# Four of eight experts with unsplit float32 weights, two products side by side on TensorE

## The chip, the cores and the metric

The kernel runs on one core of one Trainium2 chip. The metric is the time of one execution on the device in microseconds (us); before the change the median of three runs is 2477.5 us.

## What is computed

The reference is a network of two layers over 256 latent tokens with 1024 channels, behind 256 context tokens. Each layer has a normalised, modulated input, three token mixers, an output projection, and then a SwiGLU stage: dense in the first layer, eight experts of which each token takes two in the second. All arrays are float32. The change touches only the expert stage of the second layer, which works on the 256 latent tokens:

```
D_MODEL, D_FF_EXPERT, N_EXPERTS, TOP_K = 1024, 2816, 8, 2

def swiglu(h, w_gate, w_up, w_down):
    return (jax.nn.silu(h @ w_gate) * (h @ w_up)) @ w_down

def moe_swiglu(h, w_router, w_gate, w_up, w_down):
    logits = h @ w_router
    top_v, top_i = lax.top_k(logits, TOP_K)
    top_w = jax.nn.softmax(top_v, axis=-1)
    combine = jnp.sum(jax.nn.one_hot(top_i, N_EXPERTS) * top_w[..., None], axis=-2)
    out = combine[..., 0:1] * swiglu(h, w_gate[0], w_up[0], w_down[0])
    for e in range(1, N_EXPERTS):
        out = out + combine[..., e:e + 1] * swiglu(h, w_gate[e], w_up[e], w_down[e])
    return out
```

A residual with a gate row and a last norm follow.

## The kernel before

**Ranks and slots.** The router's code (from L1160 on) counts the tokens of each expert and puts the experts in the order of falling counts: rank 0 has most tokens. The counts of all ranks add up to 512. `posr` holds for each token and rank its slot, `comr` its factor, `eidi` the expert of a rank, `cnti` the counts. The kernel works by rank, with a fixed number of slots for each: 128 + 64 for rank 0, 128 for ranks 1 to 4, 64 for ranks 5 to 7.

**Float32 by split parts.** A float32 value is split into a high and a low part of a narrower type (fp32r in the profile), whose sum is the value: `split` (L111) has ScalarE (ACT) write the high part as a copy (L114) and VectorE (DVE) the low part as a difference (L115). A block of 128 slots is multiplied with a block of weights by three products on TensorE (PE): high by high, high by low of the weights, low of the tokens by high. A block of 64 slots holds both parts of its tokens side by side, 128 columns in all, so two products do: by the weights' high and by their low part. One such sweep over an expert's weights is called a pass below.

**Weights.** They lie in memory in blocks ("units") of 128 rows x 1024 float32, 512 KB: two blocks of 128 rows by 512 columns. An expert has 22 units each of gate, up and down, 66 in all, and the eight experts 528. `raw` (L117) asks for a unit on SP's DMA queue (L119) into one of six places; `weight` (L122) splits it into one of three pairs of places (`wh`, `wl`). A place is free again when its last reader is done: that of a raw unit after the split, that of a pair after PE's products.

**The order.** `slots` (L1250) gathers tokens into slots: it makes one-hot matrices on DVE, turns them on PE (L1268), and multiplies (L1279, and L1297 for rank 0's mixed block). `stream` (L1306) walks a product block by block: per block of 512 columns one PSUM bank for each slot block, per unit of weights the products of L1322, then a yield. `expert` (L1329) calls it for gate (bank names `eg`), up (`eu`) and down (`ed`); what follows the last unit of a bank is SiLU on ACT, the product with up on DVE, four transposes on PE (L1370) and a split for down; after down a split, the products that put the slots back to the tokens (L1393, "combine") and DVE's addition to the sum `eacc` (L1395). `moe` (L1198) runs ranks 1 and 2, 3 and 4, 5 and 6, and 7 through `others` (L1232). From the 264th unit on (`EVERY`), rank 0's generator is advanced by one unit after every third one of the others, and what is left of it comes last. Names in the profile carry the rank: `edr1` is the down product of rank 1, `eg0` to `ed0` are rank 0's. The scheduler keeps to the order of the code, but puts work under `prio("w")` (requests and splits of weights) far ahead and work under `prio("ev")` (what follows a finished bank) somewhat ahead. Each engine then works through its own list in order; a wait stops all that stands behind it on that engine.

**The end.** `final` (L1400) makes the residual and the norm. Then three tests (L1218, L1219) each load one count, of ranks 1, 5 and 0, and compare it with the slots of that rank; code for the surplus tokens stands behind each and is run only where there are any.

## Time and profile before

| | |
|---|---|
| three runs | 2478.45, 2477.50, 2477.01 us; median 2477.5 |
| span of the profiled execution | 2472.9 us, 33330 instructions |
| its own time | not measured apart from its span |
| PE busy | 2379.4 us, 96%, 11759 products |
| DVE busy | 1808.8 us, 73% |
| ACT busy | 1338.7 us, 54% |
| POOL busy | 20.3 us, 1% |
| DMA | 469.69 MB, 190 GB/s over the span |

The profile is of one execution; its span runs from the first to the last instruction and leaves out what lies around them, which the runs' times hold. Busy is the time in which an engine has an instruction under way; products on PE overlap in the records, so a row's duration is longer than the step to the next row. PE's granted clock is at full speed in nearly all of the span.

### The profile page before, as it was taken

Reading aid. Unit: us, or ns where it says so; the run is one execution under the profiler, and the core shown is the slowest. Engines: PE = TensorE matmul, PEld = TensorE weight load, DVE = VectorE, ACT = ScalarE, POOL = GpSimd, SP = SyncE. Lnnn points to the kernel's source line nnn. Section 1 sums busy time; section 2 is a strip of 40 time slices with the busy share of each in tenths; the row PEclk is TensorE's granted clock in tenths of the full one; section 3 lists DMA queues with packets and bytes.
Section 4 is the critical chain, followed back from the end, with each engine's and each line's share of the span. In section 5 each row is a group of like instructions: output and inputs, shape, how many; then the busy total and the mean of one; then the engine's idle time right before and its main releaser. Section 6 shows DMA issues by size and latency. Waiting matters only on the chain.

```text
span 2472.9 us, 33330 instructions
## 1 busy us (share of the span) xinstructions
PE 2379.4 (96%) x11759; PEld 1809.5 (73%) x11759; DVE 1808.8 (73%) x2655; ACT 1338.7 (54%) x2047; POOL 20.3 (1%) x30
## 2 busy tenths in 40 slices
PE   7999999999998999999999999989999999999995
PEld 3475476778787777777877789867788787767774
DVE  3285696574456677765798867688899888888986
ACT  3133454854434222223536676467777778788874
POOL 0000000000000000000000000000000000000000
PEclk9999999999999999999999999989999999999998
DMA  7533431112243555543332333479999999999994
GB/s 270 155 94 102 146 101 51 52 52 86 85 141 94 155 167 159 162 137 111 105 99 80 112 98 117 145 267 356 346 333 359 343 333 335 349 323 335 342 328 169
DMA packets 144334, 469.69 MB, mean 190 GB/s; under 512 B 15760, under 2 KB 16272, under 8 KB 144144
## 3 DMA queue, kind: packets, MB, share of 16 engines
q1 hardware_dynamic: 143296, 464.71, 54.6%
q10 hardware_dynamic: 848, 2.62, 0.3%
q8 instruction: 98, 1.61, 0.3%
q14 instruction: 92, 0.75, 0.1%
HBM read 466.22 MB, written 1.05 MB: 189 GB/s over the span
## 4 chain that ended last, share of the span: by engine, by line
PE 77%; DVE 10%; DMA 4%; ACT 4%; issue 3%; POOL 0%; SPq 0%; POOLq 0%; DVEq 0%; ACTq 0%
PE eur L1322 7%; PE edr L1322 7%; PE egr L1322 6%; DMA adaw<-in_ada_w_dram 3%; PE wg L179 3%; PE wg L181 2%; PE wg L180 2%; PE ada L318 2%; PE xbcL L180 2%; PE eu L1322 2%; PE xbcL L179 2%; PE xbcL L181 2%; PE ed L1322 1%; PE eg L1322 1%; DVE adac L343 1%
## 5 line engine op out<-in xcount | busy, mean ns | idle before, releaser
L115 DVE TENSOR_TENSOR l_eur<-r_eur,h_eur 128x1024 fp32r<-128x1024 f32 x154 | 185.4, 1221 | 27.3 <-ACT h_eur L114 26.8
L115 DVE TENSOR_TENSOR l_edr<-r_edr,h_edr 128x1024 fp32r<-128x1024 f32 x154 | 186.4, 1222 | 21.4 <-ACT h_edr L114 14.3
L115 DVE TENSOR_TENSOR l_egr<-r_egr,h_egr 128x1024 fp32r<-128x1024 f32 x154 | 186.2, 1220 | 12.0 <-ACT h_egr L114 10.2
L114 ACT ACTIVATE h_edr<-r_edr 128x1024 fp32r<-128x1024 f32 x154 | 162.3, 1059 | 52.3 <-PE edr L1322 28.1
L114 ACT ACTIVATE h_egr<-r_egr 128x1024 fp32r<-128x1024 f32 x154 | 162.3, 1059 | 31.5 <-PE eur L1322 19.1
L114 ACT ACTIVATE h_eur<-r_eur 128x1024 fp32r<-128x1024 f32 x154 | 160.7, 1056 | 23.5 <-PE egr L1322 9.7
L343 DVE SCALAR_TENSOR_TENSOR adac<-adaw,sc,adac 128x512 f32<-128x512 f32 x168 | 118.5, 746 | 41.7 <-DMA adaw<-in_ada_w_dram 41.2
L1322 PE MATMUL egr<-l_egr,gHp 128*128 128x512 f32 (+1 forms) x336 | 131.3, 393 | 4.0 <-DVE l_egr L115 3.7
L179 PE MATMUL wg<-hHm,h_wg 128*128 128x512 f32 (+1 forms) x384 | 132.5, 346 | 0.0
L1322 PE MATMUL eur<-l_eur,gHp 128*128 128x512 f32 (+1 forms) x336 | 129.0, 387 | 2.3 <-DVE l_eur L115 1.9
L181 PE MATMUL wg<-hHm,l_wg 128*128 128x512 f32 (+1 forms) x384 | 130.7, 343 | 0.1
L180 PE MATMUL wg<-hLm,h_wg 128*128 128x512 f32 (+1 forms) x384 | 130.0, 339 | 0.0
L1322 PE MATMUL egr<-h_egr,gHp 128*128 128x512 f32 (+1 forms) x336 | 125.7, 376 | 1.1 <-ACT h_egr L114 1.1
L1322 PE MATMUL edr<-l_edr,hHr 128*128 128x512 f32 x308 | 123.2, 400 | 3.0 <-DVE l_edr L115 1.7
L1322 PE MATMUL eur<-h_eur,gHp 128*128 128x512 f32 (+1 forms) x336 | 125.3, 376 | 0.7 <-ACT h_eur L114 0.7
L1322 PE MATMUL edr<-h_edr,hHr 128*128 128x512 f32 x308 | 121.3, 394 | 0.0
L115 DVE TENSOR_TENSOR l_wg<-r_wg,h_wg 128x1024 fp32r<-128x1024 f32 x48 | 58.8, 1224 | 42.9 <-ACT h_wg L114 42.1
L526 DVE SCALAR_TENSOR_TENSOR ccv<-cu,cols,ccv 128x482 f32<-128x482 f32 (+14 forms) x120 | 84.9, 729 | 0.7
L1322 PEld LDWEIGHTS egr<-l_egr,gHp 128*128 128x128 f32 x336 | 63.2, 188 | 28.7 <-DVE l_egr L115 19.7
L1322 PEld LDWEIGHTS eur<-l_eur,gHp 128*128 128x128 f32 x336 | 63.2, 188 | 26.4 <-DVE l_eur L115 16.5
L179 PEld LDWEIGHTS wg<-hHm,h_wg 128*128 128x128 f32 x384 | 72.8, 190 | 10.0 <-issue 2.8
L181 PEld LDWEIGHTS wg<-hHm,l_wg 128*128 128x128 f32 x384 | 72.4, 189 | 9.7 <-issue 1.6
(664 smaller groups left out, 6567.3 us busy)
## 6 DMA issues: line engine op xcount, KB each, us to landing
r_egr<-in_moe_gate_dram SPq DMA_DIRECT2D x154, 512.0 KB, 5.2
r_eur<-in_moe_up_dram SPq DMA_DIRECT2D x154, 512.0 KB, 5.3
r_edr<-in_moe_down_dram SPq DMA_DIRECT2D x154, 512.0 KB, 5.1
adaw<-in_ada_w_dram SPq DMA_DIRECT2D x160, 256.0 KB, 3.0
r_wg<-in_w_in_dram SPq DMA_DIRECT2D x48, 512.0 KB, 3.5
r_xbcL<-in_w_in_dram SPq DMA_DIRECT2D x24, 512.0 KB, 3.5
r_fg<-in_ffn_gate_dram SPq DMA_DIRECT2D x22, 512.0 KB, 3.4
r_fu<-in_ffn_up_dram SPq DMA_DIRECT2D x22, 512.0 KB, 3.5
```

Source lines behind the costliest of these rows:

```text
L114: nc.scalar.activation(Hd, src, AF.Copy)
L115: nc.vector.tensor_tensor(Ld, src, Hd.bitcast(F32), op=ALU.subtract)
L179: mm(out, wh, xh, start=(first and kk == 0), stop=False, skip_group_check=True)
L180: mm(out, wh, xl, start=False, stop=False, skip_group_check=True)
L181: mm(out, wl, xh, start=False, stop=(kk == kc - 1), skip_group_check=True)
L318: nc.tensor.matmul(ps[32 * j:32 * j + 32, :], self.sc[:, k, :], w[j % 2], start=(k == 0), stop=(k == KD - 1), skip_group_check=True)
L343: nc.vector.scalar_tensor_tensor(d, w, c, d, op0=ALU.mult, op1=ALU.add)
L526: nc.vector.scalar_tensor_tensor(y[:, :, a:b], x[:, :, a + s:b + s], w[:, k:k + 1], y[:, :, a:b], op0=ALU.mult, op1=ALU.add)
L1322: mm(ps[j][:, :n], st[kk], w[p][:, k, :], start=(kk == 0 and q == 0), stop=(kk == kc - 1 and q == len(ops) - 1), skip_group_check=True)
```

## The change

Ranks 4 to 7 leave the path of split weights. Rank 4 gets 64 slots in place of 128.

* `slots64` (L1274 of the changed kernel) makes and turns one-hot matrices as `slots` does, gathers all four blocks of 64 slots at once, with one product of 256 columns in place of one for each block, and keeps the tokens as float32 (`xn`).
* `expert64` (L1305) multiplies them with the raw units as they arrive, in float32 and without a split. A block of 64 tokens fills 64 columns of PE's array. So gate's product goes to the partitions 0 to 63 of one PSUM bank (name `nn`) and up's to 64 to 127, in turns; for down the two halves of the 1024 output columns take these places (`nd`). One piece of such an expert, up to a yield, is a unit of gate and one of up, or two units of down: four such half-products (eight in the two pieces of the last block of 256 columns). An expert has 33 pieces and 140 half-products, the four together 132 and 560. Behind a bank follow ACT's copy (`nt`, L1332), four transposes (`np`, L1335), SiLU (`ns`, L1338) and DVE's product; behind down a split and the combine with four additions.
* `moe` runs two generators by turns: `wide` (rank 0 first, then ranks 1, 2 and 3) and `narrow` (ranks 4 to 7). While rank 0's 66 units last, a turn is two wide units and two narrow pieces, then three and one (`TURN`).
* There are eight raw places, not six, and five PSUM banks for accumulation in place of four, which leaves three for the rest (the banks of `pw`), not four.
* The count gets a ninth column, the largest surplus over all ranks, and one outer test of it stands around the three tests.
* A scratch area for DMA gets the size 1024; the comments are dropped.

528 units are split before and 264 after. The number of units that are asked for stays 528, on the same queue. The engines' lists are the same up to the expert stage's gathers.

The diff, without the comments that it drops:

```diff
-        cn, self.cnti = tl(NE), self.cst.tile([128, NE], I32, name="cnti")
+        cn, self.cnti = tl(NE + 1), self.cst.tile([128, NE + 1], I32, name="cnti")
         nc.vector.tensor_tensor(c1, pm, cnt[:, None, :].to_broadcast(sq), op=ALU.mult)
-        nc.vector.tensor_reduce(cn, c1, axis=AX.X, op=ALU.add)
+        nc.vector.tensor_reduce(cn[:, 0:NE], c1, axis=AX.X, op=ALU.add)
+        caps = tl(NE)
+        for v, cap in ((caps[:, 0:1], 192.0), (caps[:, 1:4], 128.0), (caps[:, 4:NE], 64.0)):
+            nc.gpsimd.memset(v, cap)
+        nc.vector.tensor_tensor(caps, cn[:, 0:NE], caps, op=ALU.subtract)
+        nc.vector.tensor_reduce(cn[:, NE:NE + 1], caps, axis=AX.X, op=ALU.max)
+        nc.vector.tensor_scalar(cn[:, NE:NE + 1], cn[:, NE:NE + 1], 0.0, None, op0=ALU.max)
         nc.vector.tensor_copy(self.cnti, cn)
...
     def moe(self):
...
-        r0 = largest()
-        n = 0
-        for _ in self.others((((1, 0, 128), (2, 0, 128)), ((3, 0, 128), (4, 0, 128)), ((5, 0, 64), (6, 0, 64)), ((7, 0, 64),))):
-            n += 1
-            if n >= self.EVERY[0] and (n < self.EVERY[0] + KD or (n - self.EVERY[0]) % self.EVERY[1] == 0):
-                next(r0, None)
-        for _ in r0:
+        near = []
+        xw = []
+        for _ in self.slots("0", ((0, 0, 128), (0, 128, 64)), "g0", xw):
             pass
+        for _ in self.slots64("n", tuple((r, 0) for r in range(4, NE)), near):
+            pass
+        def wide():
+            yield from self.expert("0", 0, xw, "eh")
+            yield from self.others((((1, 0, 128), (2, 0, 128)), ((3, 0, 128),)))
+        def narrow():
+            for r, x in zip(range(4, NE), near):
+                yield from self.expert64(f"n{r}", r, x)
+        w, n = wide(), narrow()
+        left = FF // 128 * 3
+        while True:
+            a, b = self.TURN[0] if left > 0 else self.TURN[1]
+            more = [next(w, None) for _ in range(a)] + [next(n, None) for _ in range(b)]
+            left -= a
+            if all(m is None for m in more):
+                break
         self.final()
-        for lim, blocks in ((1, ((1, 128, 128), (2, 128, 128))), (5, ((5, 64, 64), (6, 64, 64))), (0, ((0, 192, 64),))):
-            cn = nc.values_load(self.cnti[0:1, lim:lim + 1], min_val=0, max_val=256)
-            with self.tc.If(cn > blocks[0][1]):
...
-    EVERY = 264, 3
+        more = nc.values_load(self.cnti[0:1, NE:NE + 1], min_val=0, max_val=256)
+        with self.tc.If(more > 0):
+            for lim, cap, blocks in ((1, 128, ((1, 128), (2, 128))), (0, 192, ((0, 192),)), (4, 64, ((4, 64), (5, 64), (6, 64)))):
+                cn = nc.values_load(self.cnti[0:1, lim:lim + 1], min_val=0, max_val=256)
+                with self.tc.If(cn > cap):
...
+    TURN = (2, 2), (3, 1)
 
...
+    def slots64(self, nm, blocks, res):
+        nc = self.nc
+        mm = nc.tensor.matmul
+        nb = len(blocks)
...
+        x = self.p8.tile([128, KD, nb * 64], F32, name=f"x{nm}", tag="xn", bufs=1)
+        for k in range(KD):
+            ps = self.pw(f"xn{nm}{k}")[:, :nb * 64]
+            for p in range(2):
+                for b in range(2):
+                    mm(ps.rearrange("p (j s) -> p j s", s=64), self.hx[p][b][:, k * 128:(k + 1) * 128], oh[b][:, :, 0],
+                       start=(p == 0 and b == 0), stop=(p == 1 and b == 1))
+            (nc.vector.tensor_copy if k % 2 else nc.scalar.copy)(x[:, k], ps)
+            yield
+        res += [([x[:, k, j * 64:(j + 1) * 64] for k in range(KD)], ohT[:, j * 256:(j + 1) * 256]) for j in range(nb)]
+    def expert64(self, nm, r, block):
+        nc = self.nc
+        mm = nc.tensor.matmul
+        fc = FF // 128
+        x, oT = block
+        e = nc.sync.value_load(self.eidi[0:1, r:r + 1], min_val=0, max_val=NE - 1)
+        def unit(t, u, s):
+            with self.prio("w"):
+                return self.raw(self.a[t][0][bass.ds(e, 1), u].rearrange("e p n -> p (e n)"), f"r_{s}{nm}{u}")
+        hT = self.p8.tile([128, fc * 64], F32, name=f"hn{nm}", tag="hn", bufs=1)
+        for c in range(-(-FF // 512)):
+            n = min(512, FF - c * 512)
+            nk = 1024 // n
+            no = n // 128
+            ps = self.acc(f"n{nm}{c}")
+            for i in range(KD // nk):
+                w = [unit(t, c * 4 + i, s).rearrange("p (k n) -> p k n", n=n) for t, s in (("moe_gate", "ng"), ("moe_up", "nu"))]
+                for k in range(nk):
+                    kk = i * nk + k
+                    for h in range(2):
+                        mm(ps[64 * h:64 * h + 64, :n], x[kk], w[h][:, k, :], start=(kk == 0), stop=(kk == KD - 1), skip_group_check=True)
+                if (i + 1) * nk == KD:
+                    with self.prio("ev"):
+                        t = self.t2(f"nt{nm}{c}")[:, :n]
+                        nc.scalar.activation(t, ps[:, :n], AF.Copy)
+                        pt = self.pw(f"np{nm}{c}")
+                        for o in range(no):
+                            nc.tensor.transpose(pt[:, o * 128:(o + 1) * 128], t[:, o * 128:(o + 1) * 128], self.con("id"))
+                        v = pt[:, :n].rearrange("p (o h s) -> p o h s", h=2, s=64)
+                        s = self.t2(f"ns{nm}{c}")[:, :no * 64].rearrange("p (o s) -> p o s", s=64)
+                        nc.scalar.activation(s, v[:, :, 0], AF.Silu)
+                        d = hT[:, c * 256:c * 256 + no * 64].rearrange("p (o s) -> p o s", s=64)
+                        nc.vector.tensor_tensor(d, v[:, :, 1], s, op=ALU.mult)
+                yield True
+        ps = self.acc(f"nd{nm}")
+        for i in range(fc // 2):
+            w = [unit("moe_down", h * (fc // 2) + i, "nd").rearrange("p (k n) -> p k n", n=512) for h in range(2)]
+            for k in range(2):
+                kk = i * 2 + k
+                for h in range(2):
+                    mm(ps[64 * h:64 * h + 64], hT[:, kk * 64:(kk + 1) * 64], w[h][:, k, :], start=(kk == 0), stop=(kk == fc - 1), skip_group_check=True)
+            if i == fc // 2 - 1:
+                with self.prio("ev"):
+                    y = [self.p2.tile([128, 512], F32R, name=f"yn{p}{nm}", tag="yn" + p, bufs=1) for p in "HL"]
+                    self.split(ps, *y)
+                    for b in range(2):
+                        pc = [self.pw(f"nc{nm}{b}{h}") for h in range(2)]
+                        for q in range(2):
+                            for h in range(2):
+                                v = slice(64 * h, 64 * h + 64)
+                                mm(pc[h], oT[v, b * 128:(b + 1) * 128], y[q][v], start=(q == 0), stop=(q == 1))
+                        for h in range(2):
+                            dst = self.ea[b][:, h * 512:(h + 1) * 512]
+                            nc.vector.scalar_tensor_tensor(dst, pc[h], self.comr[:, b, r:r + 1], dst, op0=ALU.mult, op1=ALU.add)
+            yield True
-            self.pools(st, "m", 1, 1, 6, 6, 3, 4, ohT=3)
+            self.pools(st, "m", 1, 1, 6, 8, 3, 5, ohT=3)
             self.moe()
...
-    nc = _bacc.Bacc("TRN2", target_bir_lowering=False, num_devices=1)
+    nc = _bacc.Bacc("TRN2", target_bir_lowering=False, num_devices=1, dynamic_dma_scratch_size=1024)
```

What this makes of the engines' lists, at two places. PE, before, where rank 1's down product starts (L1322 are its products; `h_` and `l_` are the parts of the weights, `hHr1` and `hLr1` those of the hidden rows; L1370 turns the last block of hidden rows):

```order
L1322 MATMUL edr10_0_13644<-h_edr10_0_13647,hHr1_13018 128x512
L1322 MATMUL edr10_0_13644<-l_edr10_0_13648,hHr1_13018 128x512
L1322 MATMUL edr10_0_13644<-h_edr10_0_13647,hLr1_13019 128x512
L1370 MATMUL etr150_13637<-con_t_96,esr150_13597 128x128 x2
L1322 MATMUL edr10_0_13644<-h_edr10_0_13647,hHr1_13018 128x512
L1322 MATMUL edr10_0_13644<-l_edr10_0_13648,hHr1_13018 128x512
L1322 MATMUL edr10_0_13644<-h_edr10_0_13647,hLr1_13019 128x512
L1322 MATMUL edr10_0_13644<-h_edr10_1_13659,hHr1_13018 128x512
```

PE, after, at the same place (L1436 is the old L1322, L1484 the old L1370; L1328 are the half-products, of rank 6, `r_ng` a raw unit of gate and `r_nu` one of up):

```order
L1436 MATMUL edr10_0_16082<-h_edr10_0_16085,hHr1_15300 128x512
L1328 MATMUL nn63_15961<-r_ngn614_16095,xn_13079 64x512
L1484 MATMUL etr150_16075<-con_t_96,esr150_16027 128x128 x2
L1436 MATMUL edr10_0_16082<-l_edr10_0_16086,hHr1_15300 128x512
L1436 MATMUL edr10_0_16082<-h_edr10_0_16085,hLr1_15301 128x512
L1436 MATMUL edr10_0_16082<-h_edr10_0_16085,hHr1_15300 128x512
L1436 MATMUL edr10_0_16082<-l_edr10_0_16086,hHr1_15300 128x512
L1436 MATMUL edr10_0_16082<-h_edr10_0_16085,hLr1_15301 128x512
L1328 MATMUL nn63_15961<-r_nun614_16097,xn_13079 64x512
L1328 MATMUL nn63_15961<-r_ngn614_16095,xn_13079 64x512
L1328 MATMUL nn63_15961<-r_nun614_16097,xn_13079 64x512
L1436 MATMUL edr10_0_16082<-h_edr10_1_16105,hHr1_15300 128x512
```

The four half-products of a piece stand by one wide product and five wide ones apart from each other: gate's first stands alone, three follow together.

PE, after, a little further, where a bank of rank 6 is full (L1335 turns it, `ntn63` is ACT's copy of it):

```order
L1436 MATMUL edr10_0_16082<-h_edr10_3_16129,hLr1_15301 128x512
L1328 MATMUL nn63_15961<-r_nun615_16141,xn_13079 64x512
L1328 MATMUL nn63_15961<-r_ngn615_16139,xn_13079 64x512
L1328 MATMUL nn63_15961<-r_nun615_16141,xn_13079 64x512
L1436 MATMUL edr10_0_16082<-h_edr10_4_16159,hHr1_15300 128x512
L1335 MATMUL npn63_16149<-con_t_96,ntn63_16147 128x128 x4
L1436 MATMUL edr10_0_16082<-l_edr10_4_16160,hHr1_15300 128x512
```

One wide product stands between the last half-product and the transposes of its bank. ACT's list at that place has the copy (L1332) behind the high parts (L114) of the weights of the units to come:

```order
L114 ACTIVATE h_edr10_2_16117<-r_edr10_2_16115 128x1024
L114 ACTIVATE h_edr10_3_16129<-r_edr10_3_16127 128x1024
L114 ACTIVATE h_edr10_4_16159<-r_edr10_4_16157 128x1024
L1332 ACTIVATE ntn63_16147<-nn63_15961 128x512
L114 ACTIVATE h_edr10_5_16171<-r_edr10_5_16169 128x1024
L1338 ACTIVATE nsn63_16154<-npn63_16149 128x256
```

SP's queue takes the requests in the same turns: behind two (later three) units for the wide experts stand the two units of each narrow piece, each request behind the release of a raw place.

## Rows read from the trace of the kernel before

**Rows 1.** The page's part 2: the span in 40 slices of 61.8 us, busy tenths of PE, its granted clock in tenths, mean busy tenths of the 16 DMA engines, and GB/s moved. The expert stage begins in slice 27.
```profile
PE   7999999999998999999999999989999999999995
...
PEclk9999999999999999999999999989999999999998
DMA  7533431112243555543332333479999999999994
GB/s 270 155 94 102 146 101 51 52 52 86 85 141 94 155 167 159 162 137 111 105 99 80 112 98 117 145 267 356 346 333 359 343 333 335 349 323 335 342 328 169
```

**Rows 2.** The table by windows, of the two halves of the expert stage: length, then busy us (and instructions) of PE, PEld, DVE, ACT and POOL, granted clock, DMA share, GB/s.
```profile
1627.00:2030.00 403.00, 400.72 (x1879) 319.40 (x1879) 361.21 (x368) 311.05 (x346) 0.00 (x0) 1.00 0.96 346
2030.00:2440.00 410.00, 394.74 (x1847) 300.13 (x1846) 363.87 (x414) 328.45 (x456) 0.00 (x0) 1.00 0.93 334
```

**Rows 3.** The timeline at the stage's two edges: start, duration, engine, line, operation. Above its first request for weights and its first product, below its last two products.
```profile
1621.48 0.36 SPq L119 DMA_DIRECT2D r_egr<-in_moe_gate_dram  x1
1621.49 0.45 PE L1268 MATMUL ohpp<-con_t,ohp 128*128 128x128 f32 x1 [3.44 <-issue]
...
2448.46 0.62 PE L1393 MATMUL ec<-yL,ohT 128*128 128x512 f32 x2
```

**Rows 4.** The chain of waits, in order of time: one unbroken piece on PE in the down product of rank 1 (start, us, count).
```profile
1695.85 15.48 PE edr L1322 x68
```

**Rows 5.** The timeline of PE around a group of four transposes in the first half of the stage (start, duration).
```profile
1665.23 0.39 PE L1322 MATMUL egr<-h_egr,gHp 128*128 128x512 f32 x1
1665.50 0.66 PE L1370 MATMUL etr<-con_t,esr 128*128 128x128 f32 x4
1665.91 0.47 PE L1322 MATMUL egr<-l_egr,gHp 128*128 128x512 f32 x1
1666.22 0.39 PE L1322 MATMUL egr<-h_egr,gLp 128*128 128x512 f32 x1
```

**Rows 6.** The groups of instructions on PE within the stage (1621 to 2449 us): transposes, gather products, combine products; count, busy us, mean ns, idle before.
```profile
L1370 PE MATMUL etr<-con_t,esr 128*128 128x128 f32 x88 | 14.8, 287 | 0.0
L1279 PE MATMUL egp<-ohp,hxH 128*128 128x256 f32 (+1 forms) x64 | 13.6, 295 | 0.0
...
L1393 PE MATMUL ecr<-yHr,ohTp 128*128 128x512 f32 x28 | 9.5, 422 | 1.4 <-ACT yHr L114 1.4
```

**Rows 7.** The waits of PE's weight loads within the stage: us in total, times, longest.
```profile
PEld egr L1322 <- DVE l_egr L115: 19.7, 53, 1.0
PEld eur L1322 <- DVE l_eur L115: 16.5, 41, 1.1
PEld edr L1322 <- DVE l_edr L115: 11.6, 24, 1.0
```

**Rows 8.** The groups of instructions on DVE and on ACT within the stage: the low part and the high part of a block of weights, and ACT's copy of a product of 512 columns.
```profile
L115 DVE TENSOR_TENSOR l_edr<-r_edr,h_edr 128x1024 fp32r<-128x1024 f32 x154 | 186.4, 1222 | 21.4 <-ACT h_edr L114 14.3 <-PE edr L1322 2.3
...
L114 ACT ACTIVATE h_edr<-r_edr 128x1024 fp32r<-128x1024 f32 x154 | 162.3, 1059 | 52.3 <-PE edr L1322 28.1 <-PE eu L1322 6.2 <-PE eg L1322 6.1
...
L1375 ACT ACTIVATE eur<-eur 128x512 f32<-128x512 f32 (+1 forms) x18 | 10.1, 560 | 6.0 <-PE eur L1322 5.7
```

**Rows 9.** The timeline of SP's DMA queue in the gate and up products of rank 2: start of a run of requests, us until the last of them, count.
```profile
1742.50 4.38 SPq L119 DMA_DIRECT2D r_egr<-in_moe_gate_dram  x4
...
1754.40 4.38 SPq L119 DMA_DIRECT2D r_egr<-in_moe_gate_dram  x4
```

**Rows 10.** The timeline of PE, the float32 products of the first modulation (32 columns of weights, in the two halves of a block of rows by turns) and of the attention (64 columns, in the two halves of the array by turns), then the attention's line as a whole. A product leaves two records.
```profile
14.41 1.91 PE L397 MATMUL ada<-adaw,sc 128*32 128x512 f32 x8
...
20.93 4.48 PE L397 MATMUL ada<-adaw,sc 128*32 128x512 f32 x18
...
206.03 0.65 PE L728 MATMUL po<-PT,vL 128*64 128x256 f32 x2
...
207.24 0.65 PE L728 MATMUL po<-PT,vL 128*64 128x256 f32 x4
...
228.53 1.08 PE L728 MATMUL po<-PT,vL 128*64 128x256 f32 x6
...
L728 PE MATMUL po<-PT,vL x160: 379/379/431, 198.4 to 1398.6; 128*64 128x256 f32 x160
```

**Rows 11.** The timeline of PE around one float32 product of the modulation (L318) among full-array products of split weights.
```profile
60.01 0.39 PE L179 MATMUL ggL<-hHm,h_ggL 128*128 128x512 f32 x1
60.33 1.05 PE L318 MATMUL ada<-adaw,sc 128*32 128x512 f32 x2
61.31 0.50 PE L180 MATMUL ggL<-hLm,h_ggL 128*128 128x512 f32 x1
61.64 0.39 PE L181 MATMUL ggL<-hHm,l_ggL 128*128 128x512 f32 x1
```

**Rows 12.** The page's part 6: requests of gate's weights, count, KB each, median us from issue to landing.
```profile
r_egr<-in_moe_gate_dram SPq DMA_DIRECT2D x154, 512.0 KB, 5.2
```

**Rows 13.** The line of the three tests at the end: the compares of SP's and ACT's queue and ACT's signals (duration min, median, max in ns; first and last start in us).
```profile
L1219 SPq COMPARE_BRANCH  x3: 45/45/53, 2457.5 to 2467.4; - x3
L1219 ACTq COMPARE_BRANCH  x3: 45/50/54, 2458.9 to 2469.7; - x3
...
L1219 ACTq EVENT_SEMAPHORE  x3: 17/17/17, 2463.3 to 2471.8; - x3
```

**Rows 14.** The timeline of DVE after the last product: the two additions of the last combine.
```profile
2448.90 1.41 DVE L1395 SCALAR_TENSOR_TENSOR eacc<-ec,comr,eacc 128x512 f32<-128x512 f32 x2 [0.60 <-PE ec L1393]
```

More of the change, by code (lines that the diff above doesn't have):

```diff
@@ L1202, in moe @@
         nc = self.nc
-        def largest():
-            g = []
-            yield from self.slots("0", ((0, 0, 128), (0, 128, 64)), "g0", g)
-            yield from self.expert("0", 0, g, "e0")
-        r0 = largest()
-        n = 0
-        for _ in self.others((((1, 0, 128), (2, 0, 128)), ((3, 0, 128), (4, 0, 128)), ((5, 0, 64), (6, 0, 64)), ((7, 0, 64),))):
-            n += 1
-            if n >= self.EVERY[0] and (n < self.EVERY[0] + KD or (n - self.EVERY[0]) % self.EVERY[1] == 0):
-                next(r0, None)
@@ L1214, in moe @@
-        for _ in r0:
-            pass
-        self.final()
-        for lim, blocks in ((1, ((1, 128, 128), (2, 128, 128))), (5, ((5, 64, 64), (6, 64, 64))), (0, ((0, 192, 64),))):
-            cn = nc.values_load(self.cnti[0:1, lim:lim + 1], min_val=0, max_val=256)
-            with self.tc.If(cn > blocks[0][1]):
-                for t in self.ea:
-                    nc.vector.memset(t, 0.0)
-                g = []
-                for _ in self.slots(f"x{lim}", blocks, "g", g):
-                    pass
-                for j, (r, _, _) in enumerate(blocks):
-                    for _ in self.expert(f"x{lim}{r}", r, [g[j]], "eh"):
-                        pass
-                self.final()
@@ new lines, in moe @@
+        w, n = wide(), narrow()
[6 more added lines that the diff above has]
+                break
+        self.final()
+        more = nc.values_load(self.cnti[0:1, NE:NE + 1], min_val=0, max_val=256)
[3 more added lines that the diff above has]
+                with self.tc.If(cn > cap):
+                    for t in self.ea:
+                        nc.vector.memset(t, 0.0)
+                    g = []
+                    if cap == 128:
+                        for _ in self.slots(f"x{lim}", tuple(b + (128,) for b in blocks), "g", g):
+                            pass
+                    else:
+                        for _ in self.slots64(f"x{lim}", blocks, g):
+                            pass
+                    for (r, _), x in zip(blocks, g):
+                        for _ in self.expert(f"x{lim}{r}", r, [x], "eh") if cap == 128 else self.expert64(f"x{lim}{r}", r, x):
+                            pass
+                    self.final()
@@ L1248, in others @@
             g = nxt
+    def slots64(self, nm, blocks, res):
+        nc = self.nc
+        mm = nc.tensor.matmul
+        nb = len(blocks)
+        oh = [self.p2.tile([128, nb, 2, 64], F32R, name=f"on{nm}{b}", tag="on", bufs=2) for b in range(2)]
+        ohT = self.p2.tile([128, nb * 256], F32R, name=f"onT{nm}", tag="onT", bufs=1)
+        for b in range(2):
+            for j, (r, s0) in enumerate(blocks):
+                nc.vector.tensor_scalar(oh[b][:, j], self.con("iota")[:, None, s0:s0 + 64].to_broadcast([128, 2, 64]),
+                                        self.posr[:, b, r:r + 1], None, op0=ALU.is_equal)
+        for j0 in range(0, nb, 2):
+            n = min(2, nb - j0)
+            pt = self.pw(f"onp{nm}{j0}")
+            for j in range(n):
+                for b in range(2):
+                    sl = slice(j * 256 + b * 128, j * 256 + (b + 1) * 128)
+                    nc.tensor.transpose(pt[:, sl], oh[b].bitcast(F32)[:, j0 + j].rearrange("p c s -> p (c s)"), self.con("id"))
+            nc.scalar.activation(ohT[:, j0 * 256:(j0 + n) * 256], pt[:, :n * 256], AF.Copy)
+        x = self.p8.tile([128, KD, nb * 64], F32, name=f"x{nm}", tag="xn", bufs=1)
+        for k in range(KD):
+            ps = self.pw(f"xn{nm}{k}")[:, :nb * 64]
+            for p in range(2):
+                for b in range(2):
+                    mm(ps.rearrange("p (j s) -> p j s", s=64), self.hx[p][b][:, k * 128:(k + 1) * 128], oh[b][:, :, 0],
[3 more added lines that the diff above has]
+        res += [([x[:, k, j * 64:(j + 1) * 64] for k in range(KD)], ohT[:, j * 256:(j + 1) * 256]) for j in range(nb)]
@@ new lines, in expert64 @@
+    def expert64(self, nm, r, block):
[43 more added lines that the diff above has]
+                    self.split(ps, *y)
+                    for b in range(2):
+                        pc = [self.pw(f"nc{nm}{b}{h}") for h in range(2)]
[6 more added lines that the diff above has]
+                            nc.vector.scalar_tensor_tensor(dst, pc[h], self.comr[:, b, r:r + 1], dst, op0=ALU.mult, op1=ALU.add)
+            yield True
@@ L1326, in stream @@
                             evac(j, c, ps[j][:, :n])
-                yield
+                yield True
     def expert(self, nm, r, blocks, eh):
```

1 line of the change is left out of this document (removed).

## The prediction, made before the changed kernel's time was known

> **What bounds the kernel now.** I read the page's slices first: in the last third of the span, the expert stage, PE stands at nine tenths or more, the clock at full speed, and the DMA row at 9 while it moves 323 to 359 GB/s [rows 1]. So the stage has two candidates at once. The windows of its two halves [rows 2] add a third: PE is 99% busy in the first half and 96% in the second, DVE 90% and 89%, and the DMA engines 96% and 93%. Next the stage's edges: its first product starts at 1621.49 us and its last two at 2448.46 [rows 3], so it takes 827 us, and 24.4 us of the span of 2472.9 follow.
>
> How much of the 827 us is PE's own work? A pass of 128 slots over one expert is 132 products of 128x512 (44 each for gate, up and down, the half-width blocks counted as halves), and 68 of them follow each other in 15.48 us, 0.2276 us each [rows 4]. Rank 0 takes five passes, ranks 1 to 4 three each, ranks 5 to 7 two each: 23 passes, 3036 products, 691 us. A group of four transposes costs 0.53 us: 0.41 from its start to the next product, and 0.12 because the products on either side start late (0.27 and 0.31 apart where 0.23 is usual) [rows 5]. The 304 transposes (rows like x88) are 76 such groups, 40 us; 72 combine products (28 + 28 + 8 + 8) at 0.2276, 16 us; the gathers (96 of 256 columns, 96 narrower ones, at some 0.12 and 0.10) 21 us, and 368 weight products of 256 columns cost 2 us over the half I counted [rows 6]. Work: 771 us. The other 56 us are stalls. The waits name them: the weight loads of gate, up and down wait 19.7 + 16.5 + 11.6 us for the low parts that DVE writes [rows 7]; each block of weights costs DVE 1.222 us and ACT 1.059 [rows 8].
>
> DMA is close behind. In the steady part of a wide expert eight blocks of 512 KB are asked for every 11.90 us, 1.49 us each [rows 9]; all 528 blocks at that pace would take 785 us. That is the transfers' upper bound, as they were not seen to be late there.
>
> **The change, part by part.** Rank 4 goes from 128 slots to 64 and joins ranks 5 to 7; all four take weights as they arrive, gate beside up (or the two halves of down's columns) in the two column halves of the array. The reference's inputs route 129, 80, 75, 74, 50, 45, 37 and 22 tokens, so nothing overflows the new blocks either.
>
> *Removed on PE:* nine passes (three of rank 4, six of ranks 5 to 7), 9 x 132 x 0.2276 = 270 us; 66 transposes, some 16 groups, 8.7 us; a third of the wide gathers, 4 us; of the 256-column surcharge 1 us. Together 284 us.
>
> *Added on PE, the products themselves:* 560 products in a half of the array. Their price comes from the float32 products that the program has already, each of which leaves two records (the attention issues 80 of them and has 160 records). In the attention one half-array product of 256 columns lasts 0.65 us, two (x4) also 0.65, three 1.08 [rows 10]: two halves do run side by side, and a round of 256 columns is 0.43. The first modulation gives 512 columns: four products (x8) take 1.91 us, nine (x18) 4.48, so three further rounds cost 2.57, 0.857 each [rows 10]. Perfectly paired, the 560 are 264 rounds. The program's order does not pair them perfectly: 57 times a gate (or first-half) product stands alone between wide products, and the remaining three of its piece take two rounds more. Walking PE's order through the two halves I count 329.5 rounds, 282 us.
>
> *Added on PE, entering and leaving:* the order has 176 runs of half-array products. One lone float32 product between wide ones shows what a visit costs [rows 11]: the wide product at 60.01 is followed at 60.33, not 60.24; the next wide one starts 0.98 later, not 0.86; and its successor 0.33 later, not 0.23. That is 0.09 + 0.13 + 0.11 = 0.33 us. 150 runs have wide products on both sides, 26 a transpose on one, for which I take half: 150 x 0.33 + 26 x 0.16 = 54 us. Here a rule speaks against the change. The Trainium skill, TensorEngine Tiling (Array Packing), section Tiling Modes, says that changing the tiling mode drains TensorE, while moving between tiles of one mode doesn't. The rows agree that a visit costs more than its product. The Trainium skill's same page, section Overview, promises up to 2x for 64 columns; by that alone, with 264 rounds and nothing for visits, the sum would come out 110 us lower than mine.
>
> PE's own work thus changes by 282 + 54 - 284 = +52 us, to 823.
>
> *Removed elsewhere:* 264 of the 528 splits: 264 x 1.222 = 323 us of DVE and 280 of ACT. DVE falls from 725 us busy in the 813 of [rows 2] to about half. This is worth at most the 56 us of stalls. Bounds of what is left: 0 and 56. I take 15, near the low end, because the DVE waits of [rows 7] go with DVE's load: 3 for a start in which 96 gather products now precede the narrow ones' 32, 7 for the 24 groups of narrow transposes, whose input ACT copies after the last half-product (0.56 us, [rows 8]) while often one wide product alone stands between, 5 for late low parts.
>
> *Transfers:* the same 528 blocks on the same queue. A split frees its slot early, a narrow block holds it until PE is through. With eight slots, not six, the slots of the last two wide blocks of a turn come free when PE ends the turn two before, which leaves a turn of 6 to 7 us, and a landing takes 5.2 [rows 12]. A turn of three wide blocks and one narrow piece is five blocks, 3 x 1.366 + 2 x 0.857 + 0.33 = 6.1 us of PE if paired, 7.3 if split up, against 5 x 1.49 = 7.4 of transfers at the present pace. So I take no cost there, but this is the cover that is thinnest.
>
> *The end:* two of three tests go. ACT's compare comes first at 2458.9 and third at 2469.7, its last signal moves from 2471.8 to the first one's 2463.3 [rows 13]: 8.5 us less. The last combine now adds four half-tiles in a row, not two, of 0.7 us each [rows 14], so about 1.5 more. Net -7. The three added DVE operations of the count come after the slots' places and delay nothing.
>
> **Sum.** The stage 827 + 52 - 56 + 15 = 838, the end 24.4 - 7 = 17.4. The span becomes 1621.5 + 838 + 17.4 = 2477 us, 4 above the profiled 2472.9. The median of the runs is 2477.5, 4.6 above the span of the profiled one, which I take for what lies around it: **2481 us**, 0.16% more. A measurement of this kernel can tell about 0.2%, 5 us, from no change, so this is no change.
>
> **The rivals.**
> *Half-products wait for their weights (slower).* The narrow blocks hold their slots until PE is done, so a slot freed late brings the next block late, and then the first half-product of a piece stands with all wide products of the turn behind it. There are 132 pieces; a wait for a weight part is now 19.7 us in 53 times, 0.37 us [rows 7]. At 132 x 0.37 that is 49 us, of which the 15 hold some 10: 2520. For it: a turn's transfers are as long as its products. Against: in the first half the queue kept that pace beside a PE that waited for DVE alone. It decides once a block lands later than the 6 to 7 us after its slot's release.
>
> *A visit costs nothing (faster).* If half-array products start while the last full ones drain, the 54 us go: 2427, and a half of it gives 2454. That the tiles of the array work independently is what the Trainium skill says, same page, section Tiling Modes. Against it stands the visit in [rows 11]; for it, that this was one product of 32 columns and not a pair. With no stall left at all (15 us less) the forecast itself gives 2466.
>
> *The halves don't run side by side here.* The 560 would cost 496 x 0.857 + 64 x 0.43 = 453 us, 171 more: 2652. The attention's x2 and x4 rows speak against it.
>
> **How the numbers follow.** The forecast, PE bound with 5 to 28 us of stalls (2471 to 2494), gets 0.45: within 0.2% (2472.5 to 2482.5) holds 0.25 of it, above 0.14, below 0.06. Waiting half-products 0.25, 2494 to 2530, all slower. Cheaper visits or no stalls 0.28, 2420 to 2471, all faster. Unpaired halves 0.02. Faster 0.34, same 0.25, slower 0.41. The range goes from 2444 to 2518: it cuts about 0.09 at either end, the whole price of the visits below and the longest waits above.
>
> **What would show it.** Right: PE above 95% busy through the stage, two half-products in 0.86 us in a steady run, 0.33 us per visit, DVE near half busy, few waits for low parts, a DMA share still at 0.9, and one compare per engine at the end. Wrong: half-products that wait for their blocks by more than 0.1 us on average; wide products that start within 0.25 us after a pair; or rounds that take more than 0.9 us.

## The result and the profile after the change

The changed kernel takes 2505.3 us (median of 4 runs) against 2477.3: ratio 1.0119, 95% interval 1.0104 to 1.0133, 28 us **slower**. Its profiled span is 2503.0 us. The forecast said 2481 and no change; the time lies inside the range of 2444 to 2518, 24 us above the forecast. It lies outside the forecast's own branch, PE bound with 5 to 28 us of stalls, which ended at 2494.

The slices of the page, as in [rows 1]:

```profile
PE   7999999999998999999999999899999999999997
...
PEclk9999999999999999999999999889999999999998
DMA  7433421112233545532322334379889899999895
GB/s 268 152 93 105 147 93 59 50 47 91 89 126 110 164 155 161 165 124 93 125 89 94 110 102 136 116 262 332 323 305 337 324 337 339 327 333 351 320 332 215
```

The windows of the stage's two halves behind its start, as in [rows 2]:

```profile
1648.00:2060.00 412.00, 407.28 (x1758) 230.21 (x1759) 161.97 (x185) 148.27 (x202) 0.00 (x0) 1.00 0.88 323
2060.00:2486.00 426.00, 417.77 (x1667) 231.94 (x1664) 231.95 (x234) 189.70 (x224) 0.00 (x0) 1.00 0.90 327
```

PE is 99% and 98% busy, DVE 39% and 54%, and the DMA share has fallen below that of [rows 2]. The candidate that these rows leave is PE's own list.

The timeline of PE, the stage's first and last product, as in [rows 3]:

```profile
1621.40 0.45 PE L1382 MATMUL ohp<-con_t,oh 128*128 128x128 f32 x1 [3.44 <-issue]
...
2485.44 0.39 PE L1358 MATMUL ncn<-ynLn,onTn 64*128 64x512 f32 x1
```

The stage takes 864.0 us from first to last product, before 827.0; the end takes 17.6, before 24.4. So the stage lost 37 us and the end gave back 7.

The timeline of PE in the up products of a rank of 128 slots: a lone half-product, wide products, and a run of three:

```profile
2014.36 0.39 PE L1436 MATMUL eur<-h_eur,gHp 128*128 128x512 f32 x1
2014.68 1.07 PE L1328 MATMUL nn<-r_ngn,xn 128*64 128x512 f32 x2
2015.68 0.50 PE L1436 MATMUL eur<-l_eur,gHp 128*128 128x512 f32 x1
2016.02 0.39 PE L1436 MATMUL eur<-h_eur,gLp 128*128 128x512 f32 x1
...
2016.71 0.39 PE L1436 MATMUL eur<-h_eur,gLp 128*128 128x512 f32 x1
2017.03 0.64 PE L1328 MATMUL nn<-r_nun,xn 128*64 128x512 f32 x1
2017.04 0.64 PE L1328 MATMUL nn<-r_ngn,xn 128*64 128x512 f32 x1
2017.51 0.59 PE L1328 MATMUL nn<-r_nun,xn 128*64 128x512 f32 x1
2017.52 0.59 PE L1328 MATMUL nn<-r_ngn,xn 128*64 128x512 f32 x1
2017.94 1.02 PE L1328 MATMUL nn<-r_nun,xn 128*64 128x512 f32 x2
2018.89 0.50 PE L1436 MATMUL eur<-h_eur,gHp 128*128 128x512 f32 x1
```

A run is a stretch of half-products with no other product between them, a visit what PE loses on entering and leaving one, and a round the time of one product in each half. Two half-products start within 0.01 us of each other; each leaves two records, and the next product of the same half starts 0.91 us after the first one of a run. The lone one takes as long as a pair: from its start to the next wide product 1.00 us, the three 1.86. The price of a visit can be read here: 0.32 from the wide product ahead to the run where 0.23 is usual, 1.00 for a round of 0.857, and 0.34 behind the first wide product, 0.35 us in all. The trace has 176 runs, 68 of one product: 38 of gate, 25 of down, 5 of up.

The waits of PE's weight loads from 1650 us on, as in [rows 7] (us, times, longest):

```profile
PEld nn L1328 <- issue: 89.9, 300, 0.4
...
PEld eur L1436 <- DVE l_eur L115: 11.6, 15, 0.9
...
PEld egr L1436 <- DVE l_egr L115: 8.5, 14, 1.1
```

No wait of a half-product for a transfer is among them; PE arrives late, not the blocks.

### The profile page after: what moved, and what is told of

Read it like the earlier page. It is cut to its first block, busy times and chain, and to the rows that moved or that the text cites. A ratio compares the mean times of both kernels' runs of the same rounds, so it can differ in the third digit from the quotient of the medians.

```text
span 2503.0 us, 31487 instructions
## 1 busy us (share of the span) xinstructions
PE 2421.3 (97%) x11521; PEld 1662.5 (66%) x11521; DVE 1484.7 (59%) x2318; ACT 1044.5 (42%) x1695; POOL 21.6 (1%) x33
## 4 chain that ended last, share of the span: by engine, by line
PE 79%; DVE 8%; DMA 7%; ACT 3%; issue 2%; POOL 0%; SPq 0%; POOLq 0%; DVEq 0%; ACTq 0%
PE nn L1328 7%; DMA adaw<-in_ada_w_dram 4%; PE eur L1436 4%; PE ndn L1348 4%; PE edr L1436 3%; PE egr L1436 3%; PE wg L179 2%; PE wg L181 2%; PE wg L180 2%; PE ada L318 2%; PE eg L1436 2%; PE ed L1436 2%; DVE adac L343 2%; PE eu L1436 2%; PE xbcL L180 2%; PE xbcL L179 2%
## 5 line engine op out<-in xcount | busy, mean ns | idle before, releaser
L1328 PE MATMUL nn<-r_ngn,xn 128*64 128x512 f32 (+1 forms) x384 | 175.3, 571 | 0.0
L1328 PE MATMUL nn<-r_nun,xn 128*64 128x512 f32 (+1 forms) x384 | 168.0, 567 | 0.0
L115 DVE TENSOR_TENSOR l_eur<-r_eur,h_eur 128x1024 fp32r<-128x1024 f32 x66 | 79.3, 1223 | 71.8 <-ACT h_eur L114 71.3
L1348 PE MATMUL ndn<-r_ndn,hnn 128*64 128x512 f32 x352 | 109.0, 606 | 0.0
L115 DVE TENSOR_TENSOR l_edr<-r_edr,h_edr 128x1024 fp32r<-128x1024 f32 x66 | 79.7, 1223 | 46.9 <-ACT h_edr L114 46.3
L115 DVE TENSOR_TENSOR l_egr<-r_egr,h_egr 128x1024 fp32r<-128x1024 f32 x66 | 79.3, 1221 | 19.3 <-ACT h_egr L114 18.9
L114 ACT ACTIVATE h_edr<-r_edr 128x1024 fp32r<-128x1024 f32 x66 | 69.0, 1057 | 42.9 <-DMA r_edr<-in_moe_down_dram 32.8
L114 ACT ACTIVATE h_egr<-r_egr 128x1024 fp32r<-128x1024 f32 x66 | 68.2, 1055 | 31.3 <-PE eur L1436 15.8
L114 ACT ACTIVATE h_eur<-r_eur 128x1024 fp32r<-128x1024 f32 x66 | 68.0, 1054 | 20.2 <-PE egr L1436 10.9
L1328 PEld LDWEIGHTS nn<-r_nun,xn 128*64 128x64 f32 x384 | 46.1, 136 | 45.8 <-issue 44.0
L1328 PEld LDWEIGHTS nn<-r_ngn,xn 128*64 128x64 f32 x384 | 43.3, 135 | 49.5 <-issue 47.4
L179 PE MATMUL xbcL<-hHm,h_xbcL 128*128 128x512 f32 (+1 forms) x192 | 75.7, 394 | 0.0
```

Of the source, the lines that this page charges most:

```text
L114: nc.scalar.activation(Hd, src, AF.Copy)
L115: nc.vector.tensor_tensor(Ld, src, Hd.bitcast(F32), op=ALU.subtract)
L179: mm(out, wh, xh, start=(first and kk == 0), stop=False, skip_group_check=True)
L1328: mm(ps[64 * h:64 * h + 64, :n], x[kk], w[h][:, k, :], start=(kk == 0), stop=(kk == KD - 1), skip_group_check=True)
L1348: mm(ps[64 * h:64 * h + 64], hT[:, kk * 64:(kk + 1) * 64], w[h][:, k, :], start=(kk == 0), stop=(kk == fc - 1), skip_group_check=True)
```

## The experiments

Differences between experiments are taken from their ratios to the kernel before, which ran beside each of them.

**E1: the pieces kept together.** In both loops of `expert64`:

```diff
-                    for h in range(2):
+                    for h in (1, 0):
```

> The changed kernel, but the half-product of the second half (up, or down's second 512 columns) is issued before that of the first half (gate). Its weights are asked for last, so the scheduler can no longer put one half-product of a piece alone ahead of the other three. In PE's list the runs of half-products fall from 176 to 127, the rounds of 512 columns from 329.5 to 264. Theory 1 (the changed kernel loses its time where pieces are split: a lone half-product costs a whole round and a visit of its own): 65.5 x 0.857 + 49 x 0.33 = 72 us less, about 2433 us. Theory 2 (the half-products are held by transfers, and PE's list does not matter): the 528 blocks at 1.49 us each set the end, no better than 2455 us. Theory 3 (a lone one costs nothing beside the wide products): 2505 us.

2442.6 us, ratio 0.986 (0.9843 to 0.9876): 64 us less than the changed kernel, and faster than before. The same work in PE's timeline, where a piece is now one run:

```profile
1994.08 0.39 PE L1436 MATMUL eur<-h_eur,gLp 128*128 128x512 f32 x1
1994.39 0.64 PE L1328 MATMUL nn<-r_nun,xn 128*64 128x512 f32 x1
1994.40 0.64 PE L1328 MATMUL nn<-r_ngn,xn 128*64 128x512 f32 x1
...
1996.26 0.50 PE L1436 MATMUL eur<-h_eur,gHp 128*128 128x512 f32 x1
```

Four half-products take 1.87 us; split as one and three they took 1.00 + 1.86 and a second visit. From the starts of PE's records, the time in half-products falls from 310.8 to 250.0 us, 61 us of the 64. Theory 1 holds, with 64 us in place of its 72; theory 2 (no better than 2455) and theory 3 are out.

**E2: the narrow gather first.**

```diff
-        for _ in self.slots("0", ((0, 0, 128), (0, 128, 64)), "g0", xw):
-            pass
         for _ in self.slots64("n", tuple((r, 0) for r in range(4, NE)), near):
             pass
+        for _ in self.slots("0", ((0, 0, 128), (0, 128, 64)), "g0", xw):
+            pass
```

> The changed kernel with the two gathers at the start of the expert stage exchanged: first the products of 256 columns for ranks 4 to 7, then those of 128 and 64 columns for rank 0. Theory 1 (PE's clock stays at its lower level for some 20 us of the stage because the products of 128 and 64 columns come first, and everything in that time takes twice as long): the lower level ends within 5 us and some 8 us go, 2497 us. Theory 2 (the lower level has nothing to do with the order of the gathers, or it comes back in rank 0's gather): 2505 us.

2505.3 us, ratio 1.0118 (1.0101 to 1.0135): nothing. The clock is at 0.94 from 1627 to 1635 us, where it was 0.50, but falls again within rank 0's gather (0.74 from 1635 to 1648), and the first half-product starts at 1648.2 instead of 1647.9. So the lower level ends early, as theory 1 has it, and comes back in rank 0's gather, as theory 2 has it: the products of 128 and 64 columns run at full clock until PE waits 1.40 us for ACT, and at 0.50 behind that wait.

```profile
1631.80:1637.20 5.40, 5.40 (x52) 5.40 (x50) 1.03 (x4) 3.20 (x9) 0.00 (x0) 1.00 1.02 415
1639.00:1645.00 6.00, 5.94 (x22) 5.46 (x23) 1.65 (x7) 1.71 (x8) 0.00 (x0) 0.50 0.28 91
```

```profile
1639.06 1.07 PE L1411 MATMUL eg<-oh,hxH 128*128 128x128 f32 x4 [1.40 <-ACT gP L1415]
```

**E3: no turns.**

```diff
-        while True:
...
+        for _ in w:
+            pass
+        for _ in n:
+            pass
```

> The changed kernel without turns: all wide experts, then all narrow ones. Runs of half-products fall from 176 to 34, rounds from 329.5 to 265. If only PE counted: 55 + 47 us less than 2505, 2403 us. If the narrow part is bound by its transfers, as I think: the wide part takes some 484 us with its start, to about 2105, the narrow part 256 blocks at 1.40 to 1.49 us, 358 to 381 us, and the end 20: 2485 to 2508 us, with a DMA share near 1 and PE at 60% in the narrow part.

2467.8 us, ratio 0.9965 (0.9953 to 0.9978). Windows of its wide and its narrow part:

```profile
1648.00:2092.00 444.00, 443.87 (x2126) 362.15 (x2126) 357.28 (x366) 313.72 (x366) 0.00 (x0) 1.00 0.85 299
2092.00:2446.00 354.00, 328.02 (x1289) 108.62 (x1287) 31.74 (x52) 31.22 (x59) 0.00 (x0) 1.00 1.00 394
```

The narrow part is bound by its transfers, as expected: the DMA share is 1.00, and the half-products' weight loads wait 114 us for blocks. But the blocks come at 394 GB/s, 1.33 us for 0.524 MB, so the kernel is 17 us faster than my lowest figure. PE is busy for 93% of that part, not the 60% that I expected; a half-product that runs alone counts as busy too. Turns as the change takes them cost more than the transfers that they hide.

**E4: the tests alone,** in the kernel before: the count's ninth column, and

```diff
+        more = nc.values_load(self.cnti[0:1, NE:NE + 1], min_val=0, max_val=256)
+        with self.tc.If(more > 0):
...
```

> The kernel before, with the ninth column of the count and one outer test around the three, and nothing else of the change. Theory 1 (the two further tests lie on the path at the end): 8.5 us less, 2469 us, with one compare on each queue. Theory 2 (the tests lie beside the store of the output): 2477 us.

2468.6 us, ratio 0.9969 (0.9957 to 0.998): 7.5 us less, where 8.5 were expected. Theory 1 holds.

**E5 and E8: other turns,** both on E1:

```diff
-    TURN = (2, 2), (3, 1)
+    TURN = (4, 4), (6, 2)
```

> The kernel of the experiment with up first, with turns of twice the length: four units and four pieces, then six and two. Runs of half-products fall from 127 to 88, the rounds stay 264. Theory 1 (a visit costs its 0.35 us: 0.09 before, 0.15 behind, 0.11 at the next wide product): 39 x 0.35 = 14 us less than 2443, 2429 us. Theory 2 (a longer turn holds all eight raw places, so the wide units' transfers come late): no gain or a loss, 2443 to 2460 us, with DMA share down and waits of DVE and ACT for r_e blocks up. Theory 3 (PE loses nothing on a visit): 2443 us with the transfers as they were.

For E8 the pair is `(1, 1), (3, 1)`.

> The kernel of the experiment with up first, with turns of one unit and one piece while rank 0 lasts (then three and one as before): 153 runs of half-products in place of 127, the rounds nearly the same (266 for 264). By the price of a visit, 26 x 0.35 + 2 x 0.86 = 11 us more, 2454 us. If the visits cost nothing: 2445 us. If shorter turns help the transfers more than that: below 2443.

E5: 2425.0 us, ratio 0.9799 (0.978 to 0.9817); E8: 2453.4, ratio 0.991 (0.9893 to 0.9927). Against E1 that is 15 us less for 39 fewer visits and 12 us more for 26 further ones and two rounds. By 0.35 us a visit they would be 14 and 11: both agree. The loss that E5's theory 2 feared does not show.

**E7: six raw places,** on E1:

```diff
-            self.pools(st, "m", 1, 1, 6, 8, 3, 5, ohT=3)
+            self.pools(st, "m", 1, 1, 6, 6, 3, 5, ohT=3)
```

> The kernel of the experiment with up first, with six raw places in place of eight. Theory 1 (the slots are the thin cover: a narrow unit holds its place until PE is through, and a turn has five units): with six places a turn's last unit is asked for only while the turn runs, some 1 to 2 us late in each of 99 turns, 2500 us or more. Theory 2 (the queue is hidden behind PE and has room, as it reached 400 GB/s without turns): within 5 us of 2443.

2508.8 us, ratio 1.0149 (1.0122 to 1.0175): 72 us more than E1, theory 1. ACT's waits for blocks of ranks 1 to 3, first in E1, then in E7:

```profile
ACT h_edr L114 <- DMA r_edr<-in_moe_down_dram: 44.7, 36, 3.7
ACT h_egr L114 <- DMA r_egr<-in_moe_gate_dram: 19.7, 23, 3.0
ACT h_eur L114 <- DMA r_eur<-in_moe_up_dram: 15.8, 19, 2.2
```

```profile
ACT h_edr L114 <- DMA r_edr<-in_moe_down_dram: 71.5, 51, 5.0
ACT h_eur L114 <- DMA r_eur<-in_moe_up_dram: 54.7, 45, 4.5
ACT h_egr L114 <- DMA r_egr<-in_moe_gate_dram: 52.4, 47, 4.7
```

It is above all the wide blocks' splits that come late: PE itself stands still for parts of the weights of ranks 1 to 3 for 41 us, in E1 for 7. The half-products' weight loads wait for blocks for 11 us, in E1 not at all.

**E6 and E9: rank 0 last,** on E1. In E6 `wide` runs ranks 1 to 3 first, the turns of three and one come first with them, and `narrow` makes its own gather:

```diff
         def wide():
-            yield from self.expert("0", 0, xw, "eh")
             yield from self.others((((1, 0, 128), (2, 0, 128)), ((3, 0, 128),)))
+            for _ in self.slots("0", ((0, 0, 128), (0, 128, 64)), "g0", xw):
+                pass
+            yield from self.expert("0", 0, xw, "eh")
...
```

E9, on E6, spreads rank 0's gather:

```diff
-            for _ in self.slots("0", ((0, 0, 128), (0, 128, 64)), "g0", xw):
-                pass
+            then = self.slots("0", ((0, 0, 128), (0, 128, 64)), "g0", xw)
...
+                if u >= parts - FF // 128:
+                    next(then, None)
```

> The kernel of the experiment with up first, with rank 0 behind the ranks 1 to 3: the stage begins with the gather of 256 columns for ranks 1 and 2, as before the change, the narrow gather follows after the first three wide units, and rank 0's gather of 128 and 64 columns lies late in the stage. Theory 1 (the stage loses 8 to 10 us at its start because PE does the gathers of rank 0 at the clock's lower level): the first wide product comes some 10 us sooner, 2433 us. Theory 2 (that time only moves, as it did when the two gathers were exchanged): 2443 us.

> The kernel of the experiment with rank 0 last, with rank 0's gather advanced by one step of eight after each of rank 3's last 22 units of down, so that its products stand between wide ones, as before the change. Theory 1 (a block of gather products of 128 and 64 columns is done at the clock's lower level and takes 14 us where 7 are enough, wherever the block stands, and meanwhile no raw place comes free): the clock stays at full speed there, some 10 us less than 2447, about 2437 us. Theory 2 (the queue of transfers sets the pace, so PE's time there is not on the path): 2447 us.

E6: 2447.5 us, ratio 0.9891 (0.9875 to 0.9908), no gain over E1, as its theory 2 said. E9: 2435.1, ratio 0.985 (0.9832 to 0.9867), 10 us less than E6, as its theory 1 said, but not clear of E1. Windows of E6 around the gather in one block (after a stall, in it, behind it), then of E9 around the spread one:

```profile
2096.00:2100.00 4.00, 2.60 (x8) 1.48 (x9) 4.00 (x7) 0.00 (x0) 0.00 (x0) 0.58 1.00 365
2100.00:2114.00 14.00, 14.00 (x68) 14.00 (x66) 3.74 (x9) 5.06 (x16) 0.00 (x0) 0.50 0.28 99
2114.00:2124.00 10.00, 10.00 (x39) 6.06 (x39) 1.52 (x2) 1.59 (x3) 0.00 (x0) 0.85 0.23 68
```

```profile
2050.00:2073.00 23.00, 23.00 (x134) 17.00 (x131) 12.47 (x17) 12.74 (x25) 0.00 (x0) 1.00 0.93 345
```

PE stood idle before the block, the clock fell to 0.50 (1.2 GHz), and stayed there through 14 us of gather products until wide ones had run for 3 us; meanwhile no place came free and the queue idled (share 0.28). Between wide products the same gather runs at full clock: it takes 6.8 us, in E6 13.7, and the queue keeps busy (share 0.93). How the 10 us divide between the clock and the queue is not shown. Nor is it shown why E9 does not clearly beat E1. Its windows fit a gain that becomes waiting for transfers: from 1700 to 1900 us PE is busy 195 of 200 us with a DMA share of 0.99.

**E10 and E11: both together,** on E9. E10, and with `(3, 3), (9, 3)` E11:

```diff
-    TURN = (2, 2), (3, 1)
+    TURN = (4, 4), (6, 2)
```

> The same with the turns of twice the length (88 runs of half-products in place of 127). Theory 1 (both gains add): 2425 - 10 = 2415 us. Theory 2 (the transfers are the bound by then): 2425 us with a DMA share of 0.98 or more through the stage.

> The same with turns of nine units and three pieces, and three and three while rank 0 lasts: 72 runs in place of 88. By the price of a visit 16 x 0.35 = 5.6 us less than the one with double turns. If eight raw places are too few for such turns: not less than it, with more waits of PE's half-products and of ACT for blocks.

E10: 2419.1 us, ratio **0.9783** (0.9766 to 0.9801), the fastest by median, 83 us below the changed kernel, though its interval is not clear of E5's. E11: 2421.6, ratio 0.9787 (0.9771 to 0.9804), no further gain. E10 lies between its two theories, 2415 and 2425. Its DMA share is 0.99 in the first half of the stage (380 GB/s), so the transfers may be the bound there, which is not shown, and 0.89 in the second (338 GB/s), so they do not bind the whole stage. That eight places are too few for E11's turns is not shown: half-products wait for blocks for 1.7 us in it, for 1.1 in E10.

**E12: the pairs not by turns,** on E1:

```diff
-                for k in range(nk):
-                    kk = i * nk + k
-                    for h in (1, 0):
+                for h in (1, 0):
+                    for k in range(nk):
+                        kk = i * nk + k
```

> The kernel of the experiment with up first, with the half-products of a piece not by turns (up, gate, up, gate) but in blocks (up, up, gate, gate). The visits stay 127. Theory 1 (PE starts products in the order of its list, and two run side by side only where the next one in the list goes to the free half): of four in a row only the middle two overlap, three rounds in place of two, 369 rounds in place of 264, 105 x 0.857 = 90 us more, 2533 us. Theory 2 (each half works off its own products, whatever stands between): 2443 us. Theory 3 (the halves do not run side by side in blocks at all): 528 rounds, 2669 us.

2466.4 us, ratio 0.9964 (0.9952 to 0.9977): none of the three. PE's timeline of a piece in the order up, up, gate, gate:

```profile
2012.73 0.64 PE L1328 MATMUL nn<-r_nun,xn 128*64 128x512 f32 x1
2012.74 0.64 PE L1328 MATMUL nn<-r_ngn,xn 128*64 128x512 f32 x1
2013.21 0.59 PE L1328 MATMUL nn<-r_nun,xn 128*64 128x512 f32 x1
2013.22 0.59 PE L1328 MATMUL nn<-r_ngn,xn 128*64 128x512 f32 x1
```

Gate starts 0.01 us behind the first up, though by the code a second up stands between them: here each half works off its own products, as theory 2 says. The 26 us over E1 have two parts. The list again splits pieces (two up and one gate together, the last gate alone): taking for each run the longer of its two halves, there are 22 further rounds of 512 columns, 22 x 0.857 = 19 us. The runs that hold products of 256 columns, where four of one half stand in a row, take 6.5 us more. One of them:

```profile
2117.11 1.29 PE L1328 MATMUL nn<-r_nun,xn 128*64 128x256 f32 x5
2118.03 0.43 PE L1328 MATMUL nn<-r_ngn,xn 128*64 128x256 f32 x1
...
2119.90 0.50 PE L1436 MATMUL edr<-h_edr,hHr 128*128 128x512 f32 x1
```

There gate starts only 0.92 us behind the first up, together with the third, and the eight take 2.79 us where E1 takes 1.88. So theory 2 holds with two of one half in a row, not with four. The 19 and the 6.5 stand against a growth of the time in half-products by 24.4 us.

## Why the prediction was right in its range and missed the loss

The forecast was no change and the kernel is slower. "Slower" had the highest chance, 0.41, but 0.25 of it was for half-products that wait for their blocks, which did not come. The range reached past 2494 for that rival alone, so that it holds the time is in part luck. What moved the time is four terms of the sum that were all too low, 6.5, 7.2, 5.4 and 6.9 us, with nothing on the other side. The terms against the trace, each as time between starts on PE (what a wide product takes over 0.2276 us is put to its neighbour):

| term, us | forecast | measured |
|---|---|---|
| wide products | 421.6 | 421.9 |
| half-products and visits | 336 | 342.5 |
| transposes, with 7 of the waits | 39 | 39.4 |
| gathers, with 3 of the waits | 20 | 27.2 |
| combine | 16 | 21.4 |
| late low parts and the rest | 5 | 11.9 |
| stage | 838 | 864 |
| end | 17.4 | 17.6 |

- *Right:* pairs of 0.857 us, 0.33 us a visit (0.35), 176 runs, the cost of split pieces (E1), the end (E4), and DVE off the path. With 0.35 us measured for each visit, the rival of free visits fell. The Trainium skill, TensorEngine Tiling (Array Packing), section Tiling Modes, says that a change of mode drains TensorE; that each visit costs time agrees with it. The Trainium skill says in the same section that tiles work independently; E12 agrees for two products of one half in a row, and shows a limit for four.
- *Mis-sized:* the gathers were to cost 4 us less ("a third of the wide gathers") and cost 4 more. Rank 0's gather alone takes 14.2 us from start to start, before the change 7.0. The forecast priced it at full clock from a place between wide products; the change puts it at the front, in one block, where the clock is at 0.50. A window that holds it, before, and one within it, after:

```profile
2031.00:2048.00 17.00, 16.84 (x111) 14.54 (x111) 14.36 (x20) 13.59 (x30) 0.00 (x0) 1.00 0.93 320
1627.00:1635.00 8.00, 8.00 (x39) 8.00 (x39) 3.53 (x8) 3.52 (x12) 0.00 (x0) 0.50 0.99 393
```

  What of these 7 us lies on the changed kernel's path is open: in E2 this gather takes 8.8 us and a wait of 1.40, and the time is the same.
- *Left out:* the waits in the combine of the narrow ranks. What PE and its weight loads stood idle for ahead of its line, L1358 (us, times):

```profile
  DVE eacc L1361: 4.5, 4
  ACT ynHn L114: 4.4, 6
```

  It waits for DVE's additions and for ACT's split. That the three working banks cause the first was not tried.
- *Too low:* the waits and the visits, 7 us each; no run isolates these. Of the 176 runs 116 have wide products on both sides, where the forecast counted 150, and yet the trace leaves 60 us for the visits (342.5 less the 282 of the rounds), not 54. So a run beside a transpose is not entered or left at half the price.
- *Loose:* 1.49 us a block, which the forecast took as the most that the transfers need. It held as that, but E3 moved a block in 1.33, all 528 in 702 us by this pace, so the expectations of E1 and E3 that took 1.49 or 1.40 as the least were too high.
- *The rival that had the number:* half-products waiting for weights, 2494 to 2530. The time falls there, but the half-products waited for no block. The thin cover that it rested on is real: with six raw places in place of eight it is gone, as E7 shows.
- *Seen and not followed up:* the split pieces (57 by the forecast's count) stood in the sum as a fixed cost. They were the largest one to be had back: 64 us in E1.

## What to carry to other kernels

Where products share the array in halves, count the runs and rounds in the scheduled list, not the products: here a lone half cost a full round and another visit. Issue first the product whose data arrive last, so that the scheduler cannot pull one of a group ahead. And price a moved step at the clock and the cover of its new place, not of its old one: rank 0's gather took 7 us between wide products and 14 in a block.

## What the hardware showed that I had not expected

- Half-products on different column halves overlap even where the list puts two of one half in a row, but only in part with four of 256 columns in a row (E12: 2.79 us in place of 1.88).
- The clock stayed at 0.50 through 14 us of gather products of 128 and 64 columns in which PE was busy throughout (E6), and rose after 3 us of wide products. The same products ran at 1.00 for 5.4 us in E2, until PE had waited.
- The queue carried 394 GB/s over 354 us (E3), where it had moved 334 to 346 in [rows 2].
